# A mixture-of-experts layer: the experts' bias products on all 128 rows of the array

## The chip, the cores and the metric

The kernel runs on one core of a Trainium2 chip. The metric is the device time of one launch in microseconds: the median of three runs, and beside it one execution taken by the hardware profiler, whose rows are read below. The core's engines are TensorE (PE for its products, PEld for its weight loads), VectorE (DVE), ScalarE (ACT), GpSimd (POOL), and SyncE (SP), which only issues transfers here.

## What is computed

Two transformer blocks on 512 tokens of width 1024, in float32. The first has latent attention, chunked attention and a gated convolutional MLP; the second has two mixers, a mixture of 32 experts and a gated projection. The change lies in the experts: each token goes to its four best experts, and each expert applies an up projection with a bias, a clipped gated activation, and a down projection with a bias.

```python
def _moe(xt, w_router, b_router, w_up_gate, b_up_gate, w_down, b_down):
    logits = (xt @ w_router + b_router).astype(jnp.float32)
    top_vals, top_idx = lax.top_k(logits, TOP_K)
    gates = jax.nn.softmax(top_vals, axis=-1)
...
    def expert_block(args):
        xb, e = args
        hgu = xb @ w_up_gate[e] + b_up_gate[e]
        x_glu = jnp.minimum(hgu[:, :D_EXPERT], SWIGLU_LIMIT)
        x_lin = jnp.clip(hgu[:, D_EXPERT:], -SWIGLU_LIMIT, SWIGLU_LIMIT)
        hact = x_glu * jax.nn.sigmoid(SWIGLU_ALPHA * x_glu) * (x_lin + 1.0)
        return hact @ w_down[e] + b_down[e]
...
    return jnp.zeros((t, d), xt.dtype).at[slot_tok].add(ys * slot_gate[:, None].astype(xt.dtype))
```

## The kernel before

The order of all work is written out by hand: each engine takes its instructions in the order in which the code names them. The experts' stage is the loop in `moe`. A step works on the up projection of one expert, the down projection of the expert before it, and gathers rows for the next ones. An expert has a block of 128 rows of tokens; one expert, at the place TWO, has two blocks in the same pass of its weights.

**Weights.** Each expert has 12 chunks of 1 MB (eight of `w_ug`, four of `w_dn`), each 512 rows by 512 columns. A chunk is loaded by the SP queue into a tile `mraw` from a ring of eleven (pools of four, five and two). `m_ahead` splits each half chunk into a rounded part `mhi` (ScalarE) and a remainder `mlo` (VectorE), five halves ahead of their use, in a ring of six pairs. `chunk_mm` then makes, for each K tile of 128 rows, three products (`mm3`, line 171): token block's high part by `mhi`, high part by `mlo`, low part by `mhi`. The token block is the stationary operand (`xh`, `xl` for the up projection, `ah`, `al` for the down projection), the weights are the moving one, 512 columns wide; the result of 24 of them is summed in one PSUM bank.

**Biases.** `moe_open1`, some 60 us ahead of the experts' stage, puts the biases of all experts into one tile `BD` of 128 rows by 2048 columns: the up biases' high and remainder parts in rows 0 to 31 and 32 to 63, the down biases' (1024 columns only) in rows 64 to 95 and 96 to 127. The tile `E4` (`E` in the profile) has in column e a one in the rows e, 32 + e, 64 + e and 96 + e. Column e, repeated 128 times, as a stationary operand selects expert e's bias for all 128 tokens. That product opens each bank's sum, in `up` and `down` inside `expert_step`: six of them in an ordinary expert's step, with `[0:64]` for the up biases and `[64:128]` for the down biases, so that 64 of the array's rows are used:

```python
self.mm(d["u", b], d["sel"][0:64], self.BD[0:64, b * 512:(b + 1) * 512], True, False)
...
self.mm(d["d", b], d["sel"][64:128], self.BD[64:128, b * 512:(b + 1) * 512], True, False)
```

**Around them.** Between half chunks, TensorE does transposes of 128 by 128 by way of the identity in the constant tile `cst` (line 187): of the activations (`ml`), and of the next expert's gathered rows (`xg`, gathered by GpSimd from `hn_d` two steps ahead). In two of an expert's six bias products, four transposes stand just ahead. In two steps, the plan for overflowing experts makes two transposes of 32 rows (`nb`). `swap` exchanges two experts' columns of `E4`, and a loop over blocks that overflow copies one column to `selx`; in this run's data the loop is not entered.

Of the kernel before, what the change touches and what calls it, by code (L numbers as in the profile page):

```python
# [22 lines left out]
NT = 4  # L23
# [13 lines left out]
CST_PARTS = [("ident", 128), ("trin", 128), ("slow", 128), ("negm", 128), ("inv16", 16), ("inv32", 32),  # L37
             ("i32", 32), ("i128", 128), ("e4", 32), ("ule", 32), ("tok4", 4), ("ma", 128), ("mb", 128)]

# [14 lines left out]
def constants():  # L54
    p = np.arange(P)
    f = np.float32
    out = np.zeros((P, CN), f)

    def put(n, a):
        out[:, COFF[n][0]:COFF[n][1]] = a  # L60

    put("ident", np.eye(P))
    put("trin", -(p[:, None] >= p[None, :]).astype(f))
    put("slow", (p[:, None] < p[None, :]).astype(f))
    put("negm", np.where(p[:, None] >= p[None, :], f(NEG), f(0)))
    put("inv16", np.power(f(10000.0), -np.arange(16, dtype=f) / f(16)).astype(f)[None])
    put("inv32", np.power(f(10000.0), -np.arange(32, dtype=f) / f(32)).astype(f)[None])
    put("i32", np.arange(32)[None])
    put("i128", p[None])
    put("e4", (p[:, None] % 32) == np.arange(32)[None])  # L70
    put("ule", p[:, None] <= np.arange(32)[None])
    put("tok4", p[:, None] + 128 * np.arange(4)[None])
    ma = np.zeros((P, P), f)
    ma[0] = (p < 64)
    mb = np.zeros((P, P), f)
    mb[0] = np.where(p >= 64, f(NEG), f(0))
    put("ma", ma)
    put("mb", mb)
    lg = np.log(f(1.0) - np.exp2(-5.0 - np.arange(8, dtype=f)).astype(f)).astype(f)
    diff = (np.arange(512)[None, :] - p[:, None]).astype(f)  # L80
    dec = np.where(diff >= 0, np.exp(lg[:, None, None] * np.maximum(diff, f(0))), f(0)).astype(f)
    return out, np.ascontiguousarray(dec.transpose(1, 0, 2))
# [47 lines left out]
class Halves:  # L130
    """Eight blocks of columns in two tiles."""

# [8 lines left out]
class Kernel:  # L141
# [36 lines left out]
    def warm(self, n):  # L178
        """Keeps the tensor engine's clock up while it waits for data."""
        if n:  # L180
            ps = self.ps()
            for _ in range(n):
                self.mm(ps[:, 0:P], self.ones, self.ones, True, True)
# [210 lines left out]
    def norm_finish(self, x, xn, ss):  # L394
        """Rows scaled by one over their root mean square."""
        nc = self.nc
        s1 = self.sm.tile([P, NT], F32, name="ns1")
        nc.vector.tensor_tensor(s1, ss[:, :, 0], ss[:, :, 1], op=OP.add)
        r = self.sm.tile([P, NT], F32, name="nr")
        self.rstd(r, s1, D)  # L400
        for t in range(NT):
            if t % 2:
                nc.vector.tensor_scalar(xn[:, t, :], x[:, t, :], r[:, t:t + 1], None, op0=OP.mult)
            else:
                nc.scalar.activation(xn[:, t, :], x[:, t, :], AF.Copy, scale=r[:, t:t + 1])
# [5 lines left out]
    def h_block(self, x, j, scale, bias=None):  # L411
        """One block of columns of x, transposed and scaled, in two parts."""
        nc = self.nc
# [12 lines left out]
    def h_pair(self, x, j, scale, h, l):  # L426
        """As h_block, in tiles of its own."""
        nc = self.nc
        ps = self.ps()
        for t in range(NT):  # L430
            self.T(ps[:, t * P:(t + 1) * P], x[:, t, j * P:(j + 1) * P])
        nc.scalar.activation(h, ps, AF.Copy, scale=scale)
        nc.vector.scalar_tensor_tensor(l, ps, scale, h, op0=OP.mult, op1=OP.subtract)
        return h, l
# [35 lines left out]
    def zeros(self, dst):  # L470
        """Clears what transpose_masked leaves: each head's columns have zeros in the rows of its pair's other one."""
        v = dst.rearrange("p (a b) n -> p a b n", b=2)
# [98 lines left out]
    def block1(self, cg):  # L571
# [19 lines left out]
        with ExitStack() as cx:  # L591
# [44 lines left out]
            def ada(j, m, warm=0):  # L636
                """Columns of the modulation: the first m K tiles on the vector engine."""
                w = wa.pop(j)
# [668 lines left out]
    def router_weights(self):  # L1307
        """Loaded ahead of the router: its weights in two parts and its bias."""
        nc, A, pool = self.nc, self.A, self.big
# [103 lines left out]
    def overflow_blocks(self, rp):  # L1413
        """How many blocks beyond its first each expert has."""
        nc = self.nc
# [5 lines left out]
    def plan(self, rp):  # L1421
        """In steps: which expert's second block shares its weights' pass and the order of the experts that follows
        from it (that expert and TWO change places); the blocks beyond, with their experts, first ranks and places."""
        nc, nb = self.nc, self.nb
# [60 lines left out]
    def swap(self, rp):  # L1485
        """The columns of TWO and of the expert whose second block shares its weights' pass change places."""
        nc = self.nc
        e = nc.values_load(self.order[0:1, NE:NE + 1], engines=[mybir.EngineType.DVE], min_val=SWAP, max_val=NE - 1)
        def at(x):
            return (self.posm[:, :, x].rearrange("p t o -> p (t o)"),  # L1490
                    self.R[:, :, x, :].rearrange("p t o c -> p (t o) c"), self.E4[:, x])

        w = (rp.tile([P, NT], F32, name="sw0"), rp.tile([P, NT, 2], F32, name="sw1"), rp.tile([P, 1], F32R, name="sw2"))
        a, b = at(bass.ds(e, 1)), at(slice(TWO, TWO + 1))
# [4 lines left out]
    def gather_onehot(self, d):  # L1499
        """One where a row's number is the token's rank, as the positive part of one less their distance."""  # L1500
        nc = self.nc
# [6 lines left out]
    def gather_table(self, d, a=0, b=2):  # L1508
        """The token (from one) and the gate of each of the block's rows."""
        ps = self.ps()  # L1510
# [6 lines left out]
    def first_rows(self, d, hn):  # L1517
        """The first block's rows, transposed, by products with its one-hot matrix."""
        d["x"] = self.hl_tile("x", d)
# [41 lines left out]
    def m_next(self):  # L1561
        """Parts of the next half chunk (two K tiles); the splits run m_la halves ahead."""
        self.m_ahead()
# [45 lines left out]
    def expert_step(self, cur=(), prev=(), pp=(), nxt=(), extra=None):  # L1609
        """The twelve weight chunks of a step: up products of `cur`'s blocks, down products of `prev`'s, rows of `nxt`'s."""  # L1610
        nc = self.nc
# [3 lines left out]
        def up(b, c):  # L1615
# [3 lines left out]
            def mm(h):  # L1619
                def f():  # L1620
                    w = self.m_next()
                    for d in cur:
                        if c == 0 and h == 0:
                            d["u", b] = self.ps()
                            self.mm(d["u", b], d["sel"][0:64], self.BD[0:64, b * 512:(b + 1) * 512], True, False)
                        self.chunk_mm(d["x"], d["u", b], w, 2 * c + h)
# [3 lines left out]
        def down(b, c):  # L1630
# [3 lines left out]
            def mm(h):  # L1634
                def f():
                    w = self.m_next()
                    for d in prev:
                        if c == 0 and h == 0:
                            d["d", b] = self.ps()
                            self.mm(d["d", b], d["sel"][64:128], self.BD[64:128, b * 512:(b + 1) * 512], True, False)  # L1640
                        self.chunk_mm(d["a"], d["d", b], w, 2 * c + h)
# [82 lines left out]
    def moe_open(self, cx):  # L1724
        """The first expert weights, and the gain of the router's norm."""
        A = self.A
# [14 lines left out]
    def moe_open1(self, cx):  # L1741
        """Ring of expert weights, the biases in two parts and what selects an expert's."""
        nc, A = self.nc, self.A
# [3 lines left out]
        self.BD = m1.tile([P, 2048], F32R, name="BD")  # L1747
        self.E4 = m1.tile([P, NE], F32R, name="E4")
        self.cnt = m1.tile([NE, 1], F32, name="cnt")
        nc.vector.tensor_copy(self.E4, self.cc("e4"))  # L1750
        t = self.mrawA.tile([P, 4, 512], F32, name="mraw").rearrange("p a b -> p (a b)")
# [12 lines left out]
    def expert(self, e):  # L1764
        return dict(pos=lambda t: self.posm[:, t, e:e + 1], rt=lambda t: self.R[:, t, e, :],
                    sel=self.E4[:, e:e + 1].to_broadcast([P, P]))

# [10 lines left out]
    def moe(self):  # L1778
# [4 lines left out]
        self.ma = self.pool("ma", 2, ctx=cx)  # L1783
        selx = m1.tile([P, 1], F32R, name="selx")
        bs = m1.tile([P, 1], F32, name="bs")
# [3 lines left out]
        def dynamic(ej, j):  # L1789
            nc.vector.tensor_copy(bs, self.extb[:, bass.ds(j, 1)])  # L1790
            nc.vector.tensor_copy(pcx, self.posm[:, :, bass.ds(ej, 1)].rearrange("p t o -> p (t o)"))
            nc.vector.tensor_copy(rx, self.R[:, :, bass.ds(ej, 1), :].rearrange("p t o c -> p (t o) c"))
            nc.vector.tensor_copy(selx, self.E4[:, bass.ds(ej, 1)])
            nc.vector.tensor_scalar(pcx, pcx, bs, None, op0=OP.add)
# [4 lines left out]

        xd = dict(pos=lambda t: pcx[:, t:t + 1], rt=lambda t: rx[:, t, :], sel=selx.to_broadcast([P, P]))  # L1800
        ex = self.ex
# [105 lines left out]
    def ple_proj(self, c, pool):  # L1907
        """A half of the columns of p_2 times its projection."""
        ph = self.ph
# [136 lines left out]
```

## Time and profile before

| | |
|---|---|
| median of three runs | 2452.74 us (2452.15 to 2453.5) |
| profiled execution, first to last instruction | 2452.3 us |
| TensorE products, busy | 2419.6 us (99%) |
| TensorE weight loads, busy | 1843.8 us (75%) |
| VectorE, busy | 1815.7 us (74%) |
| ScalarE, busy | 1517.4 us (62%) |
| before the experts' stage | 0 to 1065 us |
| experts' stage | 1065 to 2377 us |
| last projection | 2377 to 2452 us |

An engine's busy time is the time covered by its instructions. Products are pipelined and their ends are modelled, so a product's row can be longer than the distance to the next one's start, and starts tell more than durations. A weight load has a row of its own, and its idle time is put down to what ended it; "issue" means that nothing which the profile shows was waited for.

### The profile page before, as it was taken

To read this page: it belongs to the slowest core of one execution; us is meant where nothing else is said; L and a number is where in the kernel's file an instruction comes from. 1 tells how busy PE (TensorE), PEld (TensorE's weight loads), DVE (VectorE), ACT (ScalarE), POOL (GpSimd) and SP (SyncE) were. 2 spreads that over 40 slices of the span, in tenths; PEclk is the share of its full clock that TensorE was granted. 3 is DMA by queue.
4 is the path that set the end of the run, shared out by engine and by line. 5 is a ranking of instruction groups with operands and counts; after the bars stand their busy time and mean duration, and the time that the engine had idled before them with its cause. 6 is when DMAs were issued, how large, how long until landed. Compare 5 with 4: busy or idle time off the path is not lost. (4 is left out here: it accounts for less than half of the span.)

```text
span 2452.3 us, 30624 instructions
## 1 busy us (share of the span) xinstructions
PE 2419.6 (99%) x10796; PEld 1843.8 (75%) x10796; DVE 1815.7 (74%) x2575; ACT 1517.4 (62%) x2201; POOL 164.2 (7%) x108
## 2 busy tenths in 40 slices
PE   8999999999999999989999999999999999999999
PEld 8874688888887475777777777777777777777777
DVE  5876666565556475489888888876888889888874
ACT  3676443334444157467777777855677777777764
POOL 0100000000000000020101010100101010101010
PEclk8999999999999999999999999999999999999999
DMA  9230433342333121579999999877999999999852
GB/s 316 85 126 14 142 105 111 120 121 94 95 113 103 35 68 53 183 259 331 327 335 315 338 321 339 295 254 240 332 337 322 336 321 323 338 326 322 298 190 103
DMA packets 282924, 538.66 MB, mean 220 GB/s; under 512 B 16277, under 2 KB 41397, under 8 KB 282576
## 3 DMA queue, kind: packets, MB, share of 16 engines
q1 hardware_dynamic: 268432, 508.21, 59.6%
q0 software_dynamic: 11792, 26.12, 4.0%
q10 hardware_dynamic: 2544, 2.34, 0.3%
q8 instruction: 86, 1.41, 0.2%
q14 instruction: 70, 0.57, 0.1%
HBM read 530.60 MB, written 23.59 MB: 226 GB/s over the span
## 5 line engine op out<-in xcount | busy, mean ns | idle before, releaser
L194 DVE TENSOR_TENSOR mlo<-mraw,mhi 128x1024 fp32r<-128x1024 f32 x777 | 926.0, 1223 | 181.2 <-ACT mhi L191 173.1
L191 ACT ACTIVATE mhi<-mraw 128x1024 fp32r<-128x1024 f32 x777 | 799.6, 1054 | 203.5 <-PE ps L171 181.6
L171 PE MATMUL ps<-mhi,xh 128*128 128x512 f32 x1024 | 422.7, 413 | 0.0
L171 PE MATMUL ps<-mhi,xl 128*128 128x512 f32 x1024 | 404.4, 395 | 0.0
L171 PE MATMUL ps<-mlo,xh 128*128 128x512 f32 x1024 | 403.6, 394 | 0.0
L171 PEld LDWEIGHTS ps<-mhi,xh 128*128 128x128 f32 x1024 | 192.7, 188 | 67.7 <-issue 30.1
L194 DVE TENSOR_TENSOR wlo<-raw,whi 128x1024 fp32r<-128x1024 f32 (+2 forms) x128 | 152.6, 1203 | 111.2 <-ACT whi L191 110.9
L171 PEld LDWEIGHTS ps<-mhi,xl 128*128 128x128 f32 x1024 | 192.5, 188 | 45.5 <-DVE xl L1596 0.3
L171 PEld LDWEIGHTS ps<-mlo,xh 128*128 128x128 f32 x1024 | 193.1, 189 | 37.3
L191 ACT ACTIVATE whi<-raw 128x1024 fp32r<-128x1024 f32 (+2 forms) x128 | 132.3, 1042 | 131.6 <-PE ps L171 131.2
L171 PE MATMUL ps<-mhi,ah 128*128 128x512 f32 x512 | 211.7, 414 | 0.0
L171 PE MATMUL ps<-mhi,al 128*128 128x512 f32 x512 | 202.3, 395 | 0.0
L171 PE MATMUL ps<-mlo,ah 128*128 128x512 f32 x512 | 202.3, 395 | 0.0
L171 PE MATMUL ps<-whi,hh 128*128 128x512 f32 (+1 forms) x464 | 183.8, 396 | 5.1 <-ACT hh L191 2.4
L171 PE MATMUL ps<-wlo,hh 128*128 128x512 f32 (+1 forms) x464 | 180.8, 390 | 1.9 <-DVE wlo L194 1.9
L171 PE MATMUL ps<-whi,hl 128*128 128x512 f32 (+1 forms) x464 | 180.5, 389 | 0.0
L171 PE MATMUL ps<-hh,whi 128*128 128x512 f32 x352 | 137.8, 392 | 0.0
L171 PE MATMUL ps<-hh,wlo 128*128 128x512 f32 x352 | 137.0, 389 | 0.0
L171 PE MATMUL ps<-hl,whi 128*128 128x512 f32 x352 | 137.0, 389 | 0.0
L1649 ACT ACTIVATE mg<-mg 128x512 f32<-128x512 f32 x66 | 41.7, 632 | 130.2 <-DVE mg L1648 130.2
L171 PEld LDWEIGHTS ps<-mhi,ah 128*128 128x128 f32 x512 | 96.2, 188 | 34.4 <-issue 15.1
L171 PEld LDWEIGHTS ps<-mhi,al 128*128 128x128 f32 x512 | 96.3, 188 | 23.2
(486 smaller groups left out, 3743.1 us busy)
## 6 DMA issues: line engine op xcount, KB each, us to landing
mraw<-in_w_ug SPq DMA_DIRECT2D x256, 1024.0 KB, 6.2
mraw<-in_w_dn SPq DMA_DIRECT2D x128, 1024.0 KB, 6.6
raw<-in_w_up SPq DMA_DIRECT2D x44, 512.0 KB, 3.6
raw<-in_w_in SPq DMA_DIRECT2D x40, 512.0 KB, 3.7
wa<-in_w_ada SPq DMA_DIRECT2D x12, 1024.0 KB, 9.4
raw<-in_w_ada SPq DMA_DIRECT2D x24, 512.0 KB, 4.6
raw<-in_w_down SPq DMA_DIRECT2D x22, 512.0 KB, 3.5
raw<-in_w_out SPq DMA_DIRECT2D x16, 512.0 KB, 4.8
```

The costliest lines, as they stand in the source:

```text
L171: self.nc.tensor.matmul(out, l, r, start=start, stop=stop, skip_group_check=True)
L191: self.nc.scalar.activation(hi, raw, AF.Copy)
L194: self.nc.vector.tensor_tensor(lo, raw, hi, op=OP.subtract)
L1649: nc.scalar.activation(g, g, AF.Silu, scale=1.702)
```

## The change

`E4` becomes two selecting columns for each expert: one with the ones in the upper 64 rows and exact zeros in the other half, and one the other way round. Both products of biases then use all 128 rows of `E4` and `BD`. Since the up biases' columns 1024 to 2047 had nothing in rows 64 to 127 of `BD`, that part is filled with zeros. `swap` and the overflow loop copy two numbers a row instead of one. Beside that, two unused blocks of 128 columns leave the constant tile `cst`, and doc strings go, so that line numbers shift.

```diff
-             ("i32", 32), ("i128", 128), ("e4", 32), ("ule", 32), ("tok4", 4), ("ma", 128), ("mb", 128)]
+             ("i32", 32), ("i128", 128), ("e4", 32), ("ule", 32), ("tok4", 4)]
...
-                    self.R[:, :, x, :].rearrange("p t o c -> p (t o) c"), self.E4[:, x])
+                    self.R[:, :, x, :].rearrange("p t o c -> p (t o) c"),
+                    self.E4[:, :, x].rearrange("p i o -> p (i o)"))
...
-                            self.mm(d["u", b], d["sel"][0:64], self.BD[0:64, b * 512:(b + 1) * 512], True, False)
+                            self.mm(d["u", b], d["sel"](0), self.BD[:, b * 512:(b + 1) * 512], True, False)
...
-                            self.mm(d["d", b], d["sel"][64:128], self.BD[64:128, b * 512:(b + 1) * 512], True, False)
+                            self.mm(d["d", b], d["sel"](1), self.BD[:, b * 512:(b + 1) * 512], True, False)
...
-        self.E4 = m1.tile([P, NE], F32R, name="E4")
+        self.E4 = m1.tile([P, 2, NE], F32R, name="E4")
...
-        nc.vector.tensor_copy(self.E4, self.cc("e4"))
+        for i in range(2):
+            ps = slice(64 * i, 64 * i + 64)
+            nc.vector.tensor_copy(self.E4[ps, i, :], self.cc("e4")[ps])
+            ps = slice(64 - 64 * i, 128 - 64 * i)
+            nc.vector.tensor_scalar(self.E4[ps, i, :], self.cc("e4")[ps], 0.0, None, op0=OP.mult)
+        zs = self.BD[64:128, D:2048]
+        nc.vector.tensor_scalar(zs.rearrange("p (a b) -> p a b", b=P), self.ones[64:128, None, :].to_broadcast([64, 8, P]),
+                                0.0, None, op0=OP.mult)
...
-                    sel=self.E4[:, e:e + 1].to_broadcast([P, P]))
+                    sel=lambda i: self.E4[:, i, e:e + 1].to_broadcast([P, P]))
...
-        selx = m1.tile([P, 1], F32R, name="selx")
+        selx = m1.tile([P, 2], F32R, name="selx")
...
-            nc.vector.tensor_copy(selx, self.E4[:, bass.ds(ej, 1)])
+            nc.vector.tensor_copy(selx, self.E4[:, :, bass.ds(ej, 1)].rearrange("p i o -> p (i o)"))
```

TensorE has the same 9137 rows of instructions in the same order before and after. The one place where instructions are added is VectorE's, in `moe_open1`. There `sl` and `hl` are remainders of the stage ahead, `E_8109` is the selecting tile, `BD` the biases, and `wlo` the next weights' remainder. Before:

```order
L194 TENSOR_TENSOR sl_8064<-sa,sh_8063 128x512
L194 TENSOR_TENSOR hl<-ps,hh 128x512
L1750 CAST E_8109<-cst 128x32
L1757 TENSOR_TENSOR BD<-mraw,BD 32x2048
L1757 TENSOR_TENSOR BD<-mraw,BD 32x1024
L194 TENSOR_TENSOR wlo<-raw,whi 128x1024 x4
```

And after the change:

```order
L188 TENSOR_TENSOR hl<-ps,hh 128x512
L1747 CAST E_8109<-cst 64x32
L1749 TENSOR_SCALAR E_8109<-cst 64x32
L1747 CAST E_8109<-cst 64x32
L1749 TENSOR_SCALAR E_8109<-cst 64x32
L1751 TENSOR_SCALAR BD<-ones 64x1024
L1759 TENSOR_TENSOR BD<-mraw,BD 32x2048
L1759 TENSOR_TENSOR BD<-mraw,BD 32x1024
L188 TENSOR_TENSOR wlo<-raw,whi 128x1024 x4
```

One copy has become four instructions of half its rows, and the zeros of `BD` are written ahead of the two subtractions.

## Rows read from the trace of the kernel before

**Rows 1.** The page's first line: the profiled execution's span.

```profile
span 2452.3 us, 30624 instructions
```

**Rows 2.** Busy us (instructions) of each engine: experts' stage, one step; clock, DMA, GB/s.

```profile
core 0: us, PE busy (x) PEld busy (x) DVE busy (x) ACT busy (x) POOL busy (x), PEclk, DMA share, GB/s
1065.00:2377.00 1312.00, 1311.15 (x5720) 998.06 (x5719) 1129.67 (x1246) 976.24 (x1189) 123.35 (x69) 1.00 0.90 314
1208.69:1248.56 39.87, 39.87 (x175) 30.39 (x174) 34.97 (x38) 30.49 (x38) 3.85 (x2) 1.00 0.96 330
```

**Rows 3.** Weight loads' waits, 1060 to 2377 us: us in total, times, longest.

```profile
PEld ps L171 <- issue: 105.8, 388, 0.4
PEld ps L171 <- ACT ohp L1506: 1.2, 2, 0.9
```

**Rows 4.** Bias products' weight loads: ns min/median/max, first and last start, rows by columns.

```profile
L171 PEld LDWEIGHTS ps<-BD,E x198: 182/182/183, 1065.2 to 2376.0; 64*128 64x128 f32 x198
```

**Rows 5.** TensorE in order of time around a bias product: start us, us, instruction.

```profile
1519.73 0.39 PE L171 MATMUL ps<-mlo,xh 128*128 128x512 f32 x1
1519.96 0.40 PE L171 MATMUL ps<-mhi,xl 128*128 128x512 f32 x1
1520.29 0.50 PE L171 MATMUL ps<-BD,E 64*128 64x512 f32 x1
1520.72 0.50 PE L171 MATMUL ps<-mhi,xh 128*128 128x512 f32 x1
1521.05 0.39 PE L171 MATMUL ps<-mlo,xh 128*128 128x512 f32 x1
```

**Rows 6.** TensorE after four transposes, with a bias product and without one.

```profile
1208.16 0.60 PE L187 MATMUL ps<-cst,xg 128*128 128x128 f32 x4
1208.69 0.50 PE L171 MATMUL ps<-BD,E 64*128 64x512 f32 x1
1209.12 0.50 PE L171 MATMUL ps<-mhi,ah 128*128 128x512 f32 x1
1209.45 0.40 PE L171 MATMUL ps<-mlo,ah 128*128 128x512 f32 x1
...
1212.02 0.60 PE L187 MATMUL ps<-cst,xg 128*128 128x128 f32 x4
1212.37 0.48 PE L171 MATMUL ps<-mhi,ah 128*128 128x512 f32 x1
1212.69 0.40 PE L171 MATMUL ps<-mlo,ah 128*128 128x512 f32 x1
```

**Rows 7.** TensorE around two transposes of 32 rows.

```profile
2054.27 0.40 PE L171 MATMUL ps<-mhi,xl 128*128 128x512 f32 x1
2054.60 0.23 PE L171 MATMUL ps<-cst,nb 32*16 32x32 f32 x2
2054.76 0.50 PE L171 MATMUL ps<-mhi,xh 128*128 128x512 f32 x1
2055.10 0.39 PE L171 MATMUL ps<-mlo,xh 128*128 128x512 f32 x1
```

**Rows 8.** Products by form, 400 to 985 us: busy us, mean ns, idle before.

```profile
L171 PE MATMUL ps<-hh,whi 128*128 128x512 f32 x256 | 100.4, 392 | 0.0
L171 PE MATMUL ps<-hh,wlo 128*128 128x512 f32 x257 | 100.0, 389 | 0.0
```

**Rows 9.** A later step, as rows 2; weight loads from the page: KB, us to landing.

```profile
2085.48:2125.35 39.87, 39.87 (x176) 30.38 (x175) 34.97 (x37) 30.48 (x38) 4.00 (x3) 1.00 0.99 346
...
mraw<-in_w_ug SPq DMA_DIRECT2D x256, 1024.0 KB, 6.2
```

**Rows 10.** VectorE in `moe_open1`, in order of time; in brackets idle time before.

```profile
990.16 0.17 DVE L1750 CAST E<-cst 128x32 fp32r<-128x32 f32 x1
996.16 3.54 DVE L1757 TENSOR_TENSOR BD<-mraw,BD 32x2048 fp32r<-32x2048 f32 x2 [5.83 <-ACT BD L1755]
```

**Rows 11.** A gather's issue on GpSimd; all gathers' time to landing, in us.

```profile
1166.95 1.30 POOL L1545 DMA_INDIRECT xg<-hn_d,ix  x1 [26.79 <-issue]
...
DMA to landing us min/median/max: 5.4/6.8/9.2
```

## What is expected of the change

> **What bounds the kernel now.** The order of reading was: the busy shares, the busy time by stage, the weight loads' waits, then single products in order of time. The execution spans 2452.3 us [rows 1], and 1312 us of it, from 1065 to 2377, are the experts' stage, where TensorE is busy for 1311.15 us while VectorE is at 1129.67 and ScalarE at 976.24 [rows 2]. One expert's step is 39.87 us long, with TensorE busy in all of it, VectorE for 34.97, ScalarE for 30.49 [rows 2]. So TensorE sets this stage's pace. A busy TensorE is not yet one at its best, though: its weight loads stand still for 105.8 us before 388 of them, and the releaser is "issue", that is, no other engine; the longest wait for another engine totals 1.2 us [rows 3]. What "issue" hides is seen product by product. Ordinary products of 128 rows by 512 columns start 0.23 us apart (1519.73, 1519.96). Then the bias product, which uses 64 rows, starts only 0.33 us after, at 1520.29, the next 128-row product 0.43 after that, and the one behind it 0.33 later, at 1521.05 [rows 5]. There are 198 bias products [rows 4], six in an ordinary expert's step.
>
> **The change, part by part.** *The bias product.* From the last ordinary start ahead of it to the second one behind it, 1521.05 - 1519.96 = 1.09 us pass [rows 5]. Three equal steps of 0.23 would be 0.69, so a 64-row bias product costs 0.40 us beyond its own place. Two of an expert's six stand behind four transposes. There, from the first transpose at 1208.16 to the second weight product at 1209.45 is 1.29 us; the same without a bias product, 1212.02 to 1212.69, is 0.67, and one more step of 0.23 makes 0.90, so the surplus is 0.39 [rows 6]. I take 0.39 for all of them. Is it the count of rows? The two small transposes of 32 rows in the same stage show the same pattern: 0.33 us from the product ahead (2054.27 to 2054.60), and 0.34 between the first and second 128-row products behind them (2054.76 to 2055.10) [rows 7]. The change makes every bias product a 128-row one, as its neighbours are, so I take the whole surplus away: 198 x 0.39 = 77.2 us. The bounds are 198 x 0.40 = 79.2, and nothing (below, as a rival). Nothing new runs on TensorE: as many instructions, in the same order.
>
> All of this lies on the path, since TensorE waits for nobody. Two of the waits for another engine, those for ohp that total 1.2 us [rows 3], will swallow a step of 0.39 each, since an earlier arrival only waits longer: minus 0.8, between 0 and 2. What becomes late next is looked at per expert: 39.87 - 6 x 0.39 = 37.53 us. VectorE needs 34.97 of that (93%), ScalarE 30.49 [rows 2]: close, but under. The transfers are the closest, and stand below as a rival.
>
> *Filling the selecting tile and the zeros.* VectorE gets four small instructions for one, and one that writes 64 x 1024 zeros. The old copy took 0.17 us, and two subtractions of 2048 and 1024 columns took 3.54, hence some 1.15 for 1024 columns [rows 10]. The three extra small ones are 0.5, the zeros between 0.17 and 1.77 (half of 3.54); together some 1.7 us, at most 2.3. What hides them is the 5.83 us for which VectorE sits idle just before the subtractions, waiting for ScalarE [rows 10]. Without that cover they would cost those 1.7 us once. Should ScalarE's copies of the biases have to wait for the zeros, they would start at about 990.16 + 0.17 + 1.7 = 992.0, and the subtractions' wait ends at 996.16 anyway. I count zero.
>
> *Selecting columns that are two wide.* The exchange of two experts' columns and the overflow loop's copy move two numbers a row for one: an instruction of at most 0.17 us either way [rows 10], zero.
>
> *A shorter constant tile.* 256 of its columns go, 128 x 256 x 4 bytes = 131 kB, from the first transfer of the program's queue, ahead of x. At the highest rate in the rows, 346 GB/s [rows 9], that is 0.38 us. It is worth between nothing and that; I take 0.2 off.
>
> **Sum.** 77.2 - 0.8 + 0.2 = 76.6 us off the profiled 2452.3 gives 2375.7. The median of the runs shown, 2452.74, is 0.4 above that span, so the time is 2376.1.
>
> **The rivals.** *The transfers become the bound.* An expert's step moves 330 GB/s x 39.87 us = 13.16 MB [rows 2]; in 37.53 us that is 351 GB/s. The fullest step in the trace moved 346 GB/s with the DMA share at 0.99 [rows 9], so for this speaks that the demand is above anything seen in this stage. Were 346 a ceiling, a step would last 38.0 us, 0.5 too long, 16 us over 32 experts: 2392. Against it speaks the ring. Eleven tiles of 1 MB, one used every 39.87 / 12 = 3.32 us, come round in 36.5 us; a load lands 6.2 us after its issue [rows 9], and about 3.3 go by while a tile's two halves are split, so weights lie about 27 us ahead of their use. A shortfall of 16 us eats that cushion without TensorE seeing it. It takes a ceiling under 343 GB/s (13.16 MB in 37.53 + 27/32 us) to cost anything; at 338 it is 32 x 1.4 - 27 = 18 us. I give this case 2394.
>
> *The weight load of the new bias product is not hidden.* If the 128-row load could not run beside the product ahead, its 182 ns [rows 4] would lie bare: 198 x 0.18 = 36 us of the gain stay behind, 2412. Against it: all the ordinary products have loads of 128 rows and still start 0.23 us apart [rows 5]; load and product one after the other would not fit into that. The Trainium skill, "TensorE: Matmul & The Clock Gate", Part 3, speaks for this rival: it says that a weight load overlaps products in flight only where the row groups differ, which those of two 128-row products never do. By that rule the time is this rival's; the trace's starts 0.23 us apart do not agree with it.
>
> *The surplus has nothing to do with rows.* It could come with the first product of a sum (the bias product opens one), or with the selecting operand, one column repeated 128 times. Then nothing changes: 2452. Against the first: where products of another stage open a sum (always a hh,whi), the mean of all of these is 392 ns to 389 of the hh,wlo behind them, 0.8 us in all 256 [rows 8]. Against the second: the small transposes repeat no column and show the pattern too [rows 7].
>
> *Slower: the gathered rows come late.* TensorE takes its work in order, so transposes of the next expert's rows that wait for their gather would stop everything. The gather for those at 1208.16 was issued at 1166.95 [rows 6, 11], 41.2 us ahead; after the change it is 41.2 - 2.3 = 38.9. A gather that takes longer than 38.9 us costs its excess 30 times, and from 41.5 on the gain is gone. At 42: 30 x 3.1 = 93 us, 2469. Against it: the longest took 9.2 us [rows 11], and fuller DMA engines would have to make it four times longer.
>
> **How the numbers follow.** The forecast has 0.77, the transfers' case 0.12, the bare load 0.04, no connection with rows 0.05, the late gathers 0.02. The forecast's own bounds are 2452.7 - 79.2 - 0.4 = 2373 and, with 2 us swallowed and a surplus of 0.38, 2380; I leave 2 us below for what the starts' rounding hides, and take in the transfers' case up to a little beyond its 2394: 2371 to 2395, which holds some 0.85. Anything within 0.2% (4.9 us) could not be told from no change here. Faster: 0.77 + 0.12 + 0.04 = 0.93; within 0.2%: 0.05; slower: 0.02.
>
> **What would show it.** In the new trace a bias product should start 0.23 us behind the product ahead and the next 0.23 behind it; the idle time of the loads by "issue" [rows 3] should fall by more than half; an ordinary step should last 37.5 us. VectorE should be busy for 93% of a step. The prediction is wrong if a step's length is over 38 us, with loads that wait for mhi or mlo (the transfers), or if bias products still start 0.33 us late.

## The result and the profile after

| | before | after |
|---|---|---|
| median of the runs, us | 2453.12 (2452.15 to 2458.19, 4 runs) | 2368.01 (2367.36 to 2369.25, 4 runs) |
| span of the profiled execution, us | 2452.3 [rows 1] | 2365.7 |
| bias product: ns from the start ahead to its own, and on to the next | 330, 430 [rows 5] | 230, 240 |
| weight loads' idle time by "issue", us | 105.8 [rows 3] | 0.7 |
| one ordinary expert's step, us | 39.87 [rows 2] | 37.38 |

The ratio is 0.965, with a 95% interval of 0.9636 to 0.9663: faster, by 85 us. The forecast was 2376.1 in a range of 2371 to 2395; the time lies 3 us under that range.

The page's first line, then busy us of each engine (and instructions), granted clock, DMA share and GB/s, for the experts' stage and for one step, after the change:

```profile
span 2365.7 us, 30628 instructions
...
core 0: us, PE busy (x) PEld busy (x) DVE busy (x) ACT busy (x) POOL busy (x), PEclk, DMA share, GB/s
1060.00:2291.00 1231.00, 1229.11 (x5719) 1007.09 (x5718) 1111.91 (x1246) 956.07 (x1187) 124.20 (x69) 1.00 0.95 334
1202.93:1240.31 37.38, 37.38 (x176) 30.68 (x174) 34.34 (x38) 29.82 (x38) 3.86 (x2) 1.00 0.98 345
```

Against [rows 2], TensorE does the same products and is still busy in the whole step, and the step is 2.49 us shorter. VectorE is now busy for 34.34 of 37.38 us, 92%.

TensorE around a bias product, in order of time (start us, us, instruction), after:

```profile
1202.47 0.39 PE L165 MATMUL ps<-mlo,ah 128*128 128x512 f32 x1
1202.70 0.40 PE L165 MATMUL ps<-mhi,al 128*128 128x512 f32 x1
1202.93 0.40 PE L165 MATMUL ps<-BD,E 128*128 128x512 f32 x1
1203.17 0.39 PE L165 MATMUL ps<-mhi,xh 128*128 128x512 f32 x1
1203.40 0.40 PE L165 MATMUL ps<-mlo,xh 128*128 128x512 f32 x1
```

The gaps of 0.33, 0.43 and 0.33 us of [rows 5] are gone: every start stands 0.23 or 0.24 us behind the one ahead. All bias products of the kernel after (ns min/median/max, first and last start; first the weight loads, then the products):

```profile
L165 PEld LDWEIGHTS ps<-BD,E x198: 187/188/192, 1060.2 to 2290.6; 128*128 128x128 f32 x198
L165 PE MATMUL ps<-BD,E x198: 387/398/482, 1060.2 to 2290.9; 128*128 128x512 f32 x198
```

The load of twice the rows takes 188 ns instead of 182 [rows 4], and none of it shows in the starts. What the weight loads of the experts' stage wait for (us in total, times, longest), after:

```profile
PEld ps L181 <- DVE ml L1646: 1.4, 3, 0.6
PEld ps L165 <- DVE R L1399: 1.1, 1, 1.1
PEld ps L165 <- ACT ohp L1501: 0.9, 1, 0.9
PEld ps L165 <- issue: 0.7, 2, 0.4
```

The idle time by "issue" that [rows 3] showed before 388 loads is left before two. No load waits for `mhi` or `mlo`, the weights' two halves, so the transfers don't hold TensorE up.

VectorE in `moe_open1`, in order of time, after:

```profile
985.42 0.69 DVE L1751 TENSOR_SCALAR BD<-ones 64x1024 fp32r<-64x1024 f32 x1
990.84 3.53 DVE L1759 TENSOR_TENSOR BD<-mraw,BD 32x2048 fp32r<-32x2048 f32 x2 [4.73 <-ACT BD L1757]
```

The zeros take 0.69 us, and the idle time ahead of the subtractions, 5.83 us in [rows 10], is 4.73 now: it has taken up the new work. The weights' loads after (KB, us to landing), from the page:

```profile
mraw<-in_w_ug SPq DMA_DIRECT2D x256, 1024.0 KB, 7.1
```

and all gathers, from the view of their tile:

```profile
DMA to landing us min/median/max: 5.4/7.3/8.8
```

A load of 1 MB lands 0.9 us later than in [rows 9], and the longest gather 0.4 us sooner than in [rows 11].

**Where the 86.6 us between the two spans lie.** The first expert product starts at 1060.5 (before: 1065.6), so 5.1 us are gained ahead of the experts. From there to the start of the last expert product it is 1235.8 us instead of 1316.2: 80.4. The last 1.1 lie behind. The forecast had 76.4 among the experts, 0.2 ahead of them and nothing behind. What the 4 surplus us among the experts and the 5 ahead of them are is what most of the experiments ask.

### The profile page after: what moved, and what is told of

Its sections match the earlier page's. It is cut to its first block, busy times and chain, and to the rows that moved or that the text cites. A ratio compares the mean times of both kernels' runs of the same rounds, so it can differ in the third digit from the quotient of the medians.

```text
span 2365.7 us, 30628 instructions
## 1 busy us (share of the span) xinstructions
PE 2333.8 (99%) x10796; PEld 1849.6 (78%) x10796; DVE 1799.1 (76%) x2579; ACT 1498.1 (63%) x2201; POOL 165.1 (7%) x108
## 5 line engine op out<-in xcount | busy, mean ns | idle before, releaser
L188 DVE TENSOR_TENSOR mlo<-mraw,mhi 128x1024 fp32r<-128x1024 f32 x777 | 911.3, 1219 | 118.7 <-ACT mhi L185 116.0
L185 ACT ACTIVATE mhi<-mraw 128x1024 fp32r<-128x1024 f32 x777 | 786.3, 1052 | 131.4 <-PE ps L165 110.4
L165 PE MATMUL ps<-mhi,xh 128*128 128x512 f32 x1024 | 409.6, 400 | 0.0
L165 PE MATMUL ps<-mhi,ah 128*128 128x512 f32 x512 | 203.1, 397 | 0.0
L165 PEld LDWEIGHTS ps<-mlo,ah 128*128 128x128 f32 x512 | 96.3, 188 | 20.4
```

Source lines behind the costliest of these rows:

```text
L165: self.nc.tensor.matmul(out, l, r, start=start, stop=stop, skip_group_check=True)
L185: self.nc.scalar.activation(hi, raw, AF.Copy)
L188: self.nc.vector.tensor_tensor(lo, raw, hi, op=OP.subtract)
```

## The experiments

Two quantities come back in all of them. The *spacing* is the mean distance between the starts of neighbouring ordinary products, from 1200 to 1700 us of a profile, apart for those with `ah`, `al` (some 500 pairs) and those with `xh`, `xl` (some 1000). The *step* goes from an ordinary expert's first transposes to the next expert's, 39.88 us before and 37.37 after. Each ratio is against runs of the kernel before on the same chip, whose medians there were 2454.19 to 2454.51, about 1 us above the 2453.12 beside the kernel after; differences in us between kernels that ran on different chips, such as those from the kernel after, carry that uncertainty.

### Constants shorter, nothing else

```diff
 CST_PARTS = [...
-             ..., ("tok4", 4), ("ma", 128), ("mb", 128)]
+             ..., ("tok4", 4)]
```

The bias products stay on 64 rows.

> The kernel before with the one edit that its constant tile loses the 256 unused columns; the bias products stay on 64 rows. The changed kernel was 8.4 us faster than forecast: 3.5 us of it at the start, where the positions landed at 8.54 us for 12.69, some 0.18 us in every expert's step outside the bias products (about 6 us), and the rest in clock stretches. Theory A, the shorter first transfer lets the positions land earlier and VectorE's angles no longer delay the norm: the start is 3 to 4 us shorter, first transposes of x at about 16.5 us for 19.8. Theory B, the start differs by chance between executions: the positions land anywhere between 8 and 13 us, no difference of the medians over 1 us. Theory C, other addresses of the tiles behind the constants make ordinary products start closer together: a step of an ordinary expert falls from 39.88 to about 39.7 us, 5 to 6 us in all. A and C together: 2444; neither: 2453.

Measured: 2449.35 against 2454.24, ratio 0.9979 (0.997 to 0.9988), so 4.9 us off; the interval makes it 2.9 to 7.4. The step is 39.88 us and the spacing with `ah` 233.2 ns, both as before, and from the first to the last expert product it is 1316.3 us (before: 1316.2): the gain lies ahead of the experts. In the profile, which caught the slowest of the eleven runs, the first expert product starts at 1062.8, 2.9 us earlier than before, the positions land at 6.61 and the first transposes start at 17.4.

### Constants shorter, the other tiles where they were

```diff
         self.cst = self.const.tile([P, CN], F32, name="cst")
+        self.pad = self.const.tile([P, 256], F32, name="pad")
...
```

This beside the first experiment's edit.

> As the kernel before with the shorter constant tile, but an unused tile of 1 KB a row (one column of it cleared) stands behind the constants, so that all other tiles keep the addresses that they had. Theory A (the shorter transfer): the start is 3 to 4 us shorter all the same, 2449.5. Theory C (addresses): nothing of the 0.18 us a step, which stays at 39.88 us. If the kernel with the shorter tile alone has short steps and this one has not, the addresses are shown.

Measured: 2449.72, ratio 0.9981 (0.9972 to 0.999). The gain is there with the old addresses as well, so it belongs to the smaller first transfer: 4.5 to 4.9 us by the medians for 131 kB, not 0.38. The granted clock doesn't explain it: the eleven runs of the first experiment, all with a mean clock of 0.993 of full speed, average 2449.1, and the five of the kernel before beside them with the same clock 2453.2.

### The kernel after with constants of nearly the old length

```diff
-             ..., ("tok4", 4)]
+             ..., ("tok4", 4), ("ma", 112), ("mb", 112)]
```

> The changed kernel with 224 unused columns put back into its constant tile (with all 256 its memory would not hold the wider selecting tile): the first transfer is 115 kB larger than in the changed kernel. Theory A: the positions land late again, first transposes of x at about 19.5 us, 2371.5. Theory B: no difference from 2368 beyond 1 us. Theory C: the addresses are then 896 bytes off those of the changed kernel, so steps may be anything between 37.37 and 37.55 us.

Measured: 2377.14 (2373.32 to 2379.22), ratio 0.9691 (0.9678 to 0.9704), 9.1 us above the kernel after and 5.6 above the expected 2371.5. Its step is 37.57 us, 0.20 longer, and the spacing with `ah` is 233.3 ns where after has 229.3. So something in the layout changes how fast ordinary products follow one another: from the first to the last expert product it is 1241.9 us, 6.1 longer than after. Where the other 3 lie is not shown. The profile caught the fastest of the five runs (2373.32), and there the start is no later than after: the positions land at 10.35 us, the first transposes start at 17.6, not at 19.5, and the first expert product at 1059.1, 1.4 us earlier.

### The kernel before, each bias product issued twice

```diff
 self.mm(d["u", b], d["sel"][0:64], self.BD[0:64, b * 512:(b + 1) * 512], True, False)
+self.mm(d["u", b], d["sel"][0:64], self.BD[0:64, b * 512:(b + 1) * 512], False, False)
```

The same for the down biases.

> The kernel before with every 64-row bias product issued twice in a row, so that each bias is counted twice. Theory 1, the surplus belongs to the change between 64 and 128 rows, once for a pair of changes: the second product of a pair costs an ordinary step of 0.23 us, 198 x 0.23 = 46 us more, 2499. Rival, each 64-row product costs its 0.62 us: 198 x 0.62 = 123 us more, 2576. In the trace: two bias products of a pair 0.23 us apart, or 0.4 and more.

Measured: 2501.22, ratio 1.0197 (1.0181 to 1.0213), 47.0 us longer, that is 0.24 for each added product. TensorE around such a pair in this kernel (start us, us, instruction; the two bias products are one row, and 0.73 is the time of both):

```profile
1237.23 0.60 PE L187 MATMUL ps<-cst,ml 128*128 128x128 f32 x4
1237.76 0.73 PE L171 MATMUL ps<-BD,E 64*128 64x512 f32 x2
1238.42 0.50 PE L171 MATMUL ps<-mhi,xh 128*128 128x512 f32 x1
1238.76 0.39 PE L171 MATMUL ps<-mlo,xh 128*128 128x512 f32 x1
```

From the first bias product to the first product of 128 rows it is 0.66 us, where one alone takes 0.43 [rows 5]: the second costs 0.23, the place of any product. The surplus of 0.39 is paid once for the way from 128 rows to 64 and back, whether one or two products of 64 rows stand between. The Trainium skill, "TensorEngine Tiling (Array Packing)", section Key Properties, says that a change of the tiling mode drains TensorE, and one of the tile alone does not. This trace agrees in that the price goes with the change, 0.39 us for two; a drain as such isn't seen in it, and a change of the tile alone doesn't occur in these runs.

### Only the down biases on 64 rows

```diff
-self.mm(d["d", b], d["sel"](1), self.BD[:, b * 512:(b + 1) * 512], True, False)
+self.mm(d["d", b], d["sel"](1)[64:128], self.BD[64:128, b * 512:(b + 1) * 512], True, False)
```

On the kernel after; 66 of the 198 bias products go back to 64 rows.

> The changed kernel with the down biases' products back on rows 64 to 127 alone (66 of the 198), the up biases' on 128 rows. Theory 1, each product brings its own 0.39 us: 66 x 0.39 = 26 us more than the changed kernel, 2394. Rival, part of the gain hangs on there being no change of rows at all in the stage (fewer idle moments, transfers that come in step): clearly more than that, up to all of 80 us, or clearly less.

Measured: 2393.66, ratio 0.9757 (0.9742 to 0.9772), 25.7 us above the kernel after. 66 x 0.39 = 25.7. The down biases' third costs its share, so the price is the same for products on the upper and the lower 64 rows, and it adds up.

### The kernel after without bias products

> The changed kernel with the bias products left out, so the experts' biases are missing from the result. What sets the pace next? Theory, TensorE still: 198 x 0.23 = 46 us less, 2322, with an ordinary step of 36.0 us. Rival, the transfers: a step's 13.16 MB in 36.0 us is 366 GB/s, above all that was seen in the changed kernel (362), so TensorE's weight loads wait for mhi and mlo and the time stays at 2330 to 2350. VectorE would be at 34.97 of 36.0 us, 97%.

Measured: 2329.26, ratio 0.9489 (0.9474 to 0.9503), 7 us longer than expected. Of the 46 us expected among the experts, 41.2 are there in the profile; from the last expert product to the end it is 73.4 us instead of 69.4. Most of these 4 us are one wait of TensorE some 8 us behind the experts (start us, us, instruction, in brackets the idle time and its releaser), here and in the kernel after:

```profile
2269.57 5.63 PE L165 MATMUL ps<-mraw 128*128 128x512 f32 x15 [4.91 <-DVE mlo L188]
...
2306.36 5.73 PE L165 MATMUL ps<-mraw 128*128 128x512 f32 x24 [2.31 <-issue]
```

It is 2.6 us longer here. Beside it, the granted clock is at its half for 6.8 us from 2266.9, and after has no such stretch there. Why the wait is longer isn't settled. Busy time of each engine in 200 us of its experts' stage:

```profile
1300.00:1500.00 200.00, 200.00 (x937) 163.89 (x937) 189.75 (x207) 163.59 (x208) 23.12 (x12) 1.00 1.02 364
```

TensorE has no gap, with VectorE at 95% and the transfers at 364 GB/s. So 346 GB/s, the highest in the rows ahead of the prediction, is no ceiling, and in most steps the kernel after has at least 1.35 us (37.37 against 36.02) before another engine or the transfers set the pace. Not in all: five of thirty steps are only 0.2 to 1.1 us shorter than after, and among the experts TensorE's weight loads wait 4.2 us for VectorE's `ml`, where after they wait 1.4. No load waits for `mhi` or `mlo`, so it is VectorE, and not the transfers, that begins to hold TensorE up.

### The kernel before with all addresses of the kernel after

```diff
-        self.E4 = m1.tile([P, NE], F32R, name="E4")
+        self.E4 = m1.tile([P, 2 * NE], F32R, name="E4")[:, 0:NE]
```

This on the first experiment's kernel: short constants, bias products of 64 rows, and a selecting tile as wide as after, half of it unused.

> The kernel before with the shorter constant tile and, beside it, a selecting tile that is as wide as the changed kernel's, its second half unused: all bias products stay on 64 rows, but every tile of the experts' stage lies at the address that it has in the changed kernel. In the changed kernel the products with ah and al as weights start 229.0 ns apart, in the kernel before and in both kernels that only shorten the constants or put some of them back 233.2; only in the changed kernel is the distance in memory from ah to mhi 64 bytes more than a multiple of 1024 (76864), in the others 192. Theory C2, this distance sets the spacing: 229 ns here too, an ordinary step of 39.70 us for 39.88, and 2444 in all (2449.4 of the shorter constants, less 32 x 0.18). Rival, the closer spacing comes with the 128-row bias products: 233 ns, 39.88 us, 2449.

Measured: 2442.34 (2441.46 to 2442.93), ratio 0.9949 (0.9936 to 0.9963): 7.0 us below the first experiment, which differs from it in the addresses alone. From the first to the last expert product it is 1310.8 us instead of 1316.3, so 5.5 of the 7.0 lie among the experts; the rest, on another chip, is within what can't be told apart. The step is 39.70 us. A run of uninterrupted products with `ah`, `al`, its first and last product (start us, us, instruction), in the first experiment's kernel:

```profile
1266.00 0.39 PE L165 MATMUL ps<-mlo,ah 128*128 128x512 f32 x1
...
1271.13 0.39 PE L165 MATMUL ps<-mhi,al 128*128 128x512 f32 x1
```

and in this one:

```profile
1263.68 0.40 PE L165 MATMUL ps<-mlo,ah 128*128 128x512 f32 x1
...
1268.73 0.39 PE L165 MATMUL ps<-mhi,al 128*128 128x512 f32 x1
```

Each is 22 steps from product to product: 5.13 us and 5.05 us, 233 and 229.5 ns each. Nothing but the place of tiles differs. So 128 bytes more for the selecting tile shorten the ordinary products, and this share of the result has nothing to do with the bias products.

### What in an address counts: unused bytes ahead of xh and xl

```diff
         self.mo = self.pool("mo", 1, ctx=cx, side="right")
+        self.nc.gpsimd.memset(self.mo.tile([P, 176], F32, name="pad")[:, 0:1], 0.0)
```

On the kernel after: 176 columns are 704 bytes in each partition; three more kernels have 192, 640 and 64 bytes there.

> The changed kernel with an unused tile of 704 bytes a row between the weights' parts and the tiles xh and xl (one column of it cleared), which makes the distance from xh to mhi 35904 bytes for 35200, the same remainder (64) that ah now has. Theory C2: the products with xh and xl also go from 232.5 to 229 ns, 96 of them in a step, 0.3 us a step, 10 us in all: 2358. Rival, the spacing of these products doesn't hang on this distance: 2368.

> As the kernel with 704 unused bytes ahead of xh and xl, but with 192: the distance from xh to mhi is 35392 bytes, 64 more than a multiple of 256 or 512, but 576 more than one of 1024. In the trace the spacing of the products with xh and xl tells which remainder counts: 229 ns if it is that by 256 or 512, some 232.5 if it is that by 1024 or 2048.

> As before, with 640 unused bytes: the distance from xh to mhi is 35840 bytes, a multiple of 1024. If a remainder of 64 alone is good, the spacing goes back to 232 ns or above; if small remainders are good in general, it is 229 ns or below.

> The changed kernel with 64 unused bytes ahead of xh and xl: the distance from xh to mhi has the remainder 192 by 256. If the remainder decides, products with xh and xl start 233.2 ns apart, as those with ah did at 192; a step lasts 37.4 us.

Measured: 2361.18 (ratio 0.9618, 0.9604 to 0.9631) with 704 bytes, 3 us above the expected 2358; the step is 37.10 us, 0.28 shorter than after. The others, with one timed run each: 2360.74 (192), 2358.1 (640) and 2368.79 (64). The spacings go by the distance in memory from the operand that is loaded as weights (`ah` or `xh`) to `mhi`, as the compiled programs place them, and by its remainder when divided by 256 bytes:

| remainder | spacing, ns | where |
|---|---|---|
| 192 | 233.2 to 233.3 | `ah` before, and with constants of nearly the old length; `xh` with 64 bytes |
| 128 | 232.4 to 232.8 | `xh` before, after, before with after's addresses, and after without bias products |
| 64 | 229.3 to 229.6 | `ah` after, and before with after's addresses; `xh` with 704 and with 192 bytes |
| 0 | 228.0 to 228.2 | `xh` with 640 bytes; `ah` and `xh` in the next experiment |

704 and 192 differ by 512 bytes and give the same, so the remainder counts and not the distance. Nor is it the address of either operand by itself: in the first experiment and in the one just above, `ah` lies at the same address, and the spacing is 233.2 and 229.5 ns; in all four padded kernels here `mhi` lies where it does after, and the spacing with `xh` goes from 228.1 to 233.3. `mlo` keeps its place relative to `mhi` in all these kernels, so which of the two counts isn't separated. The 64 bytes, which were to make it slower, did: the spacing with `xh` rose to 233.3 ns and the step to 37.48 us. Of the change's two moves, the 1024 bytes that the constants lose leave the remainder as it was; the 128 bytes that the selecting tile gains took `ah` from 192 to 64.

### Both remainders zero

```diff
         self.cst = self.const.tile([P, CN], F32, name="cst")
+        self.nc.gpsimd.memset(self.const.tile([P, 16], F32, name="pad0")[:, 0:1], 0.0)
...
         self.mo = self.pool("mo", 1, ctx=cx, side="right")
+        self.nc.gpsimd.memset(self.mo.tile([P, 32], F32, name="pad")[:, 0:1], 0.0)
```

On the kernel after.

> The changed kernel with two unused tiles, 64 bytes a row behind the constants and 128 ahead of xh and xl, so that the distance to mhi is a multiple of 256 both from ah (76800) and from xh (35328). So far the spacing went with the remainder of this distance by 256: 233.2 ns at 192, 232.5 at 128, 229.0 to 229.5 at 64, 228.2 at 0. If the remainder decides, both kinds of products start 228.2 ns apart, an ordinary step lasts 36.95 us for 37.37, and the time is 13 us below the changed kernel's 2368: 2355. If it was the absolute addresses, the spacing may be anything from 228 to 234.

Measured: 2353.98 (2352.13 to 2354.88), ratio 0.9588 (0.9575 to 0.9601), 14.0 us below the kernel after: the fastest of all. One step of it, columns as above:

```profile
1196.45:1233.32 36.87, 36.87 (x175) 30.61 (x174) 34.27 (x38) 29.70 (x37) 3.80 (x3) 1.00 1.02 353
```

A run of products with `xh`, `xl` between two bias products, its first and last product, in the kernel after:

```profile
1284.13 0.40 PE L165 MATMUL ps<-mhi,xh 128*128 128x512 f32 x1
...
1289.49 0.40 PE L165 MATMUL ps<-mhi,xl 128*128 128x512 f32 x1
```

and in this one:

```profile
1283.19 0.39 PE L165 MATMUL ps<-mhi,xh 128*128 128x512 f32 x1
...
1288.40 0.39 PE L165 MATMUL ps<-mhi,xl 128*128 128x512 f32 x1
```

23 steps from product to product take 5.36 and 5.21 us, 6.5 ns less for each, where the mean over 500 us is 4.1 less. A step's 48 products with `ah`, `al` and 96 with `xh`, `xl` make 48 x 1.3 + 96 x 4.1 = 456 ns of the mean spacings; the steps differ by 0.44 us, and 32 of them by 14.

### What the start gains

In the profile of the kernel before, the longest wait for a transfer at the start is that of VectorE's conversion of the positions, and TensorE's first transposes follow (start us, us, instruction, in brackets the idle time and its releaser):

```profile
12.71 0.17 DVE L298 CAST pf<-pos 128x4 f32<-128x4 int32 x1 [6.93 <-DMA pos<-in_pos]
...
19.81 0.48 PE L187 MATMUL ps<-cst,xn 128*128 128x128 f32 x1 [2.79 <-ACT xn L405]
```

and after the change:

```profile
8.56 0.17 DVE L292 CAST pf<-pos 128x4 f32<-128x4 int32 x1 [3.35 <-DMA pos<-in_pos]
...
16.51 0.44 PE L181 MATMUL ps<-cst,xn 128*128 128x128 f32 x2
```

It looks as if the positions, some 4 us earlier behind a smaller first transfer, brought everything forward. Two edits of the kernel before test that. The first issues the positions' loads ahead of the vectors' on ScalarE's queue:

```diff
+        self.pos = {}
+        for n in ("pos", "pos2"): ...
         nc.scalar.dma_start(self.vec, A["vec"])
-        self.pos = {}
-        for n in ("pos", "pos2"): ...
```

> The kernel before, with its long constant tile, but the two loads of the positions ahead of the vectors' load on ScalarE's queue. Theory A2: in the kernel before, the positions land at 12.69 us, VectorE makes the angles from them ahead of the norm's factors, and the norm waits; landing by 9 us they no longer delay it. Then the first transposes of x start at about 16.5 us for 19.8 and the time is 2451 for 2454.2. Rival: the start hangs on x alone, which the shorter constants brought earlier by 0.3 to 1.6 us: no difference over 0.5 us.

Measured: 2456.39, ratio 1.0008 (0.9999 to 1.0017), so no gain. The positions landed at 5.60 us, but now the vectors were late, at 13.46; ScalarE waits for them, and VectorE for what ScalarE makes of them (`ce`), ahead of the positions:

```profile
13.72 0.17 DVE L580 TENSOR_SCALAR ce<-ce 128x8 f32<-128x8 f32 x1 [12.72 <-ACT ce L579]
...
14.25 0.16 DVE L298 CAST pf<-pos 128x4 f32<-128x4 int32 x1
```

The same edit on the kernel with 704 bytes:

> The changed kernel with 704 unused bytes ahead of xh and xl and the positions' loads first: 2361.2 if the positions' landing costs nothing any more (it was at 8.54 us in the changed kernel), 2359 to 2360 if in some executions it still does.

Measured: 2363.88, ratio 0.9635 (0.9622 to 0.9648), 2.7 us above that kernel, for the same reason (vectors at 10.62 us).

The second edit puts the angles, which need the positions, behind the norm on VectorE, in the kernel before and in the one with both remainders zero:

```diff
-        tables = self.rope_tables("pos", ...)
...
             self.norm_finish(self.x, xn, ss)
+            tables = self.rope_tables("pos", ...)
```

> The kernel before with one part of VectorE's work put in another order: the angles that need the positions come behind the norm's factors of x, so that the positions' landing can no longer delay the norm. Theory A2: first transposes of x at 16.5 to 17.5 us for 19.8, although the constants are as long as ever and the positions land at 12 us or later; 2451 for 2454.3. Rival, the start hangs on x's transfers and thus on the shorter constants alone: under 1 us.

> The changed kernel with both distances at a multiple of 256 and the norm ahead of the angles: 2355 less 0 to 1 us, as the positions land early enough in most executions of the changed kernel.

Measured: 2453.68, ratio 0.9997 (0.9988 to 1.0006), and 2358.03, ratio 0.9607 (0.9594 to 0.962), 4 us above the same kernel without it. TensorE and VectorE in the first of the two:

```profile
16.86 0.44 PE L187 MATMUL ps<-cst,xn 128*128 128x128 f32 x2 [0.41 <-ACT xn L405]
...
16.99 0.16 DVE L298 CAST pf<-pos 128x4 f32<-128x4 int32 x1
```

The first transposes did come 2.95 us earlier than before, but only 0.5 us of that is left by 36 us: VectorE still has the angles to do, and TensorE waits 1.8 us for its `htmp`. When a small load lands also differs between kernels that don't differ there: the positions land at 8.54 us after, at 11.81 with 192 bytes ahead of `xh`, with no loss in time that could be seen (first transposes at 18.9 and 16.5 us, but first expert products at 1060.5 in both). So this much is shown: 131 kB less in the first transfer are worth 4.5 to 4.9 us by the medians. By which of the waits at the start they are gained is open; that it is the positions' landing alone, theory A2, none of these four kernels bears out.

## Why the prediction missed, step by step

- **The bias products' surplus**, 0.39 us by reading [rows 5, 6], is right to the ns that can be read: the step of the kernel before with after's addresses is 39.70 us, that of after 37.37, and six bias products lie between them: 0.388 each. The cause, a change of the number of rows, is right too: paid per change in the kernel with doubled products, and by the piece with a third of them put back. From the first to the last expert product the two kernels differ by 1310.8 - 1235.8 = 75.0 us, where the forecast had 76.4.
- **That TensorE waits for nobody** held. The waits for other engines stay at a few us in the whole stage, and the weights' halves aren't among them.
- **What lies beside other work** stayed there. The zeros took 0.69 us (forecast 1.15), the four small instructions 0.16 to 0.18 each, and the idle time ahead of the subtractions shrank by 1.1.
- **A shorter constant tile** is the first step that failed. It was sized at its bytes by the rate, 0.38 us at most, and taken as 0.2; it is worth 4.5 to 4.9 in the two experiments that shorten it and keep the bias products on 64 rows. The upper bound was a rate of another stage, with nothing for what waits behind the transfer; these two experiments show that it is no bound. Through which wait the time is gained is open. The 5.1 us between the two profiles are one draw: where the constants are short and nothing else at the start is changed, the first expert product starts at 1058.1 to 1062.8 in eleven profiles, and at 1063.2 and 1065.6 in the two with the long constants.
- **The addresses** are the second: the forecast has no term for them. A wider selecting tile moves other tiles, and ordinary products with `ah` and `al` then start 3.9 ns sooner one after another; 48 of them in a step make 0.18 us, and the experts' stage 5.4 (1316.2 - 1310.8). No row of before could show that price. But the two spacings there, 233.2 ns with `ah` and 232.7 with `xh`, in products of the same form, were a hint that wasn't looked for.
- **The sum.** 75.0 + 5.4 + 5.1 + 1.1 = 86.6, the difference of the spans. The 1.1 behind the experts go with a stretch at half clock, 3.41 us at 2391.8 in the profile of before, that the one of after hasn't. Such stretches come and go between the profiles: apart from two kernels with a longer wait there, this part lasts 68.9 to 69.4 us in those without one and 70.2 to 70.8 in those with one. The forecast had 76.6, 10.0 less: 5.4 by the addresses and 5.1 - 0.2 = 4.9 by the start, minus 1.4 among the bias products, plus 1.1 behind. With the two missed amounts in its sum, 5.4 and 4.9, the forecast would have been 2365.8, and the measured 2368.0 lies 2.2 above that. Every sign that was named beforehand came out as told or nearly so (a step of 37.38 us for 37.5, VectorE at 92% for 93%). They all looked at the bias products and their step; the misses lay at the start and in 0.18 us a step, where none of the signs could show them.
- **The rivals.** *Transfers:* a step moves 345 GB/s, other kernels up to 364, a load lands after 7.1 us instead of 6.2, and no product waits. *A bare weight load:* the load of 128 rows takes 188 ns and the starts are 0.23 and 0.24 us apart. The Trainium skill's rule beside that rival in the prediction ("TensorE: Matmul & The Clock Gate", Part 3), that loads overlap only where the row groups differ, doesn't hold here; the same Part names, beside the row groups, a background weight buffer as a target that lets a load go ahead, and the prediction left that out. *No connection with the rows:* the bias product still opens the sum and still repeats a column, and the surplus is gone. *Late gathers:* the longest took 8.8 us.

## What to carry to other kernels

A product on 64 rows between products of 128 costs TensorE 0.39 us here for the way there and back, more than its own place of 0.23. Filling it with exact zeros to the neighbours' rows saves that; two such products side by side pay it once. The sign to look for is a weight load that idles by "issue". When an edit changes the size of any tile, compare the distances between the tiles that meet in the products before putting the difference down to the edit: here 128 bytes took 5.4 us off the experts' stage, and 192 bytes of padding another 14 off the whole. A transfer at the very start wasn't priced by its bytes here: 131 kB were worth over ten times the 0.38 us that their bytes make.

## What the runs showed of the hardware

- Products of 128 rows by 512 columns (float32r) at the full granted clock (1.00) started 228.0 to 233.3 ns apart, by the remainder by 256 bytes of the distance between the two operands in memory: 0 was best, 192 worst, a span of 2.3%. The rule foretold the kernel with 64 bytes and the one with both at zero. Only multiples of 64 were tried, and what in the chip makes it so is open.
- Two changes of the row count, from 128 to 64 and back, cost 0.39 us together, with one product between them or two.
- The DMA engines moved 364 GB/s over 200 us of an experts' stage beside a TensorE without gaps, at a share that the profile puts at 1.02.
